# Turning keys and queries by VectorE block transposes and DRAM transfers in place of TensorE transposes, in a hybrid attention and recurrence layer

## The chip, the core and the metric

The kernel runs on one core of a Trainium2 chip. The core has TensorE (PE in the profile; its weight loads are PEld), VectorE (DVE), ScalarE (ACT), GpSimd (POOL) and SyncE (SP), which here only issues transfers. The metric is the device time of one execution in microseconds, the median of several.

## What is computed

One layer of a hybrid encoder on 512 tokens of width 2048: a norm, one input projection, full attention with eight query and two key heads of width 128, a gated recurrence (LRU) in both directions, and an output projection with the residual. Cut to what matters here:

```python
h = rms_norm(x, norm_w)
proj = jnp.einsum('bsd,de->bse', h, w_in)
q, k, v, g_attn, xr, g_lru = jnp.split(proj, SPLITS, axis=-1)
# attention_group
q = rms_norm(q.reshape(B, S, N_HEADS, HEAD_DIM), q_norm_w)     # 8 heads of 128
k = rms_norm(k.reshape(B, S, N_KV_HEADS, HEAD_DIM), k_norm_w)  # 2 heads of 128
q, k = apply_axial_rope(q, tables), apply_axial_rope(k, tables)
s = jnp.einsum('bkgqd,bksd->bkgqs', qb, k_t) * scale           # all 512 keys
p = jax.nn.softmax(s, axis=-1)
out = jnp.einsum('bkgqs,bksd->bkgqd', p, v_t)
# hybrid_layer
mixed = concatenate([rms_norm(attn_out, attn_norm_w) * silu(g_attn),
                     rms_norm(lru_out, lru_norm_w) * silu(g_lru)], axis=-1)
return x + jnp.einsum('bse,ed->bsd', mixed, w_out)
```

Everything is float32.

## The kernel before

**Arithmetic.** Every large product is three matmuls on a high and a low part of each operand (`mm3`, L151 to L154). A high part is a rounded copy (`nc.scalar.copy`, ScalarE), a low part the difference (`nc.vector.tensor_sub`, VectorE). So for each weight tile `wr` ScalarE makes `wh` (L216) and VectorE `wl` (L217).

**Stages.** TensorE goes through the input projection in groups of 512 columns: the LRU's inputs (two groups), then keys and values (one), queries (two: heads 0 to 3, heads 4 to 7), the gates (four), and then the output projection, which a seven-product scheme computes (L906). A group takes eight chunks of weights of 512 KB; a chunk is four steps of six matmuls. The weights are loaded by SP into a ring of three. The generators of the groups are the fill: `weave(fill, chain)` takes the next n steps of the fill whenever the chain of other work yields n. TensorE's instructions stand in exactly this order; those of VectorE, ScalarE and SP are put in order by the scheduler, with priorities (`high_priority`), and in the attention SP's order is by hand too.

**Keys and queries.** A projected group is evacuated with tokens on the partitions (`evac_tok`, L513), normed and turned by rope in place (`norm_rope`, L530 to L539). The scores need the head's width on the partitions. `turn` makes that with four TensorE transposes of 128x128 into one PSUM bank (L550), and `split_ps` makes the high and low part from there (L554, L555). For the keys that happens inside the second query group, between its steps; for a query head at the first tile of the head before it, head 0 at the start of the attention.

**Attention.** `attention` runs over 32 units (8 heads, 4 tiles of 128 queries). A unit: scores in three matmuls, maximum (L600), exponential (L602), reciprocal, a product on GpSimd (L604), and a 32x32 block transpose on VectorE into `u` (L605). Every two units the block-transposed weights go to DRAM and come back in four reads, which completes the transposition (`moved`: L613 to `pd`, L620 to `pt`); then they are split into `ph` and `pl` (L624). The values of a head (L152 to L154 with `ph`, `pl` and `v`) come `NT + LATE` units after its first scores. BEGIN steps of the gates' projection go ahead of the first unit, two follow each. The projections of the gates are evacuated by L392 into `ev`.

**The LRU's sum.** `group_rstd` and `rows` turn the LRU's sum of squares into a row for all partitions: a matmul with ones (L700), a copy (L704), GpSimd, a split (L281, L282), two diagonals (L284), and a matmul (L290) that TensorE reaches four steps later, inside the second query group.

Of the kernel before, what the change touches and what calls it, by code (L numbers as in the profile page):

```python
# [11 lines left out]
F32 = mybir.dt.float32  # L12
# [5 lines left out]
P = 128  # L18
SEQ = 512
DM = 2048  # L20
KT = DM // P
NT = SEQ // P
HD = 128
NH = 8
NKV = 2
G = NH // NKV
# [16 lines left out]
WARM, WARM2 = 14, 5  # L43


BEGIN, STEPS, LATE = 10, 2, 3


H = 256


B = 32
NQ = P // B
# [9 lines left out]
def hybrid_kernel(  # L63
# [20 lines left out]
    nc = tc.nc  # L84
# [28 lines left out]
    dram = ctx.enter_context(tc.tile_pool(name="dram", bufs=1, space=bass.MemoryType.DRAM))  # L113
# [3 lines left out]
    def nm(s):  # L117
        cnt[0] += 1
        return f"{s}_{cnt[0]}"
# [10 lines left out]
    def at(tag, bufs, shape, dt=F32):  # L130
        return pools["att"].tile([P, *shape], dt, tag=tag, bufs=bufs, name=nm(tag))

    def ev(dt=F32):

        for pool, n in (("lru", 4), ("qkv", 8), ("fin", 4)):
            if pool in pools:
                return pools[pool].tile([P, SEQ], dt, tag="ev", bufs=n, name=nm("ev"))

# [3 lines left out]
    def mm():  # L142
        return ps.tile([P, SEQ], F32, tag="mm", name=nm("mm"))

    def const(shape, name, dt=F32):
        return cp.tile(list(shape), dt, tag=name, name=name)

    def f(ap):
        return ap.bitcast(F32)
# [7 lines left out]
    ident = const([P, P], "ident")  # L157
# [110 lines left out]
    def rsqrt_mean(dst, src, n, width):  # L268

        nc.gpsimd.tensor_scalar(dst, src, 1.0 / n, EPS, op0=ALU.mult, op1=ALU.add)  # L270
        last_pool[0] = nc.gpsimd.tensor_tensor(dst, dst, nhalf[:, :width], op=ALU.pow).ins
# [73 lines left out]
    def weave(fill, chain):  # L345

        for n in chain:
            for _ in range(n):
                next(fill, None)

    def drain(fill):
        for _ in fill:
            pass
# [124 lines left out]
    def lru_squares():  # L478

        hsum = pools["rot"].tile([P, 2, SEQ], F32, tag="hsum", name="hsum")  # L480
        nc.scalar.activation(hsum, hp[0], AF.Square)
        for pair in hp[1:]:
            yield 2
            sq = pools["rot"].tile([P, 2, SEQ], F32, tag="hsq", bufs=1, name=nm("hsq"))
            nc.scalar.activation(sq, pair, AF.Square)
            nc.vector.tensor_add(hsum, hsum, sq)
        sums["l"] = hsum[:, 0, :]
        nc.gpsimd.tensor_add(sums["l"], sums["l"], hsum[:, 1, :])
# [18 lines left out]
    def evac_tok(acc, tile_of):  # L507

        res = []
        with tc.high_priority():  # L510
            for t in range(NT):
                e = tile_of()
                nc.scalar.activation(e, acc[t], AF.Identity, scale=rstd[:, t : t + 1])  # L513
                res.append(e)
        return res

    def norm_rope(es, nh, tab):

        es = [e[:, : nh * HD].rearrange("p (h d) -> p h d", d=HD) for e in es]
        rs = []  # L520
        for e in es:
            r = pools["rot"].tile([P, nh], F32, tag=f"rr{nh}", bufs=NT, name=nm("rr"))
            for h in range(nh):
                sq = pools["rot"].tile([P, HD], F32, tag="sh", bufs=1, name=nm("sh"))
                nc.scalar.activation(sq, e[:, h, :], AF.Square, accum_out=r[:, h : h + 1])
            rsqrt_mean(r, r, HD, nh)
            rs.append(r)
        for t, (e, r) in enumerate(zip(es, rs)):
            sq = pools["rot"].tile([P, nh, HD], F32, tag="sq", bufs=2, name=nm("sq"))
            nc.vector.tensor_mul(e, e, r[:, :, None].broadcast_to([P, nh, HD]))  # L530
            for s in range(2):
                nc.vector.tensor_mul(
                    sq.rearrange("p h (a s d) -> p h a s d", s=2, d=32)[:, :, :, s, :],
                    e.rearrange("p h (a s d) -> p h a s d", s=2, d=32)[:, :, :, 1 - s, :],
                    tab[:, t, 1, :].rearrange("p (a s d) -> p a s d", s=2, d=32)[:, None, :, s, :]
                    .broadcast_to([P, nh, 2, 32]),
                )
            nc.vector.tensor_mul(e, e, tab[:, t, 0, :][:, None, :].broadcast_to([P, nh, HD]))
            nc.vector.tensor_add(e, e, sq)  # L539
        return es  # L540

    kth, ktl = [None] * NKV, [None] * NKV
    vh = [None] * NT
    vl = [None] * NT

    def turn(rot, h):

        pt = mm()
        for t in range(NT):
            nc.tensor.transpose(pt[:, t * P : (t + 1) * P], rot[t][:, h, :], ident)  # L550
        return pt

    def split_ps(pt, hi, lo):
        nc.scalar.copy(hi, pt)  # L554
        nc.vector.tensor_sub(lo, pt, f(hi))  # L555

    def kv(es):
        rot = norm_rope(es, NKV, rk)
        yield 20
        opened("wx", "right")  # L560
        for t in range(NT):
            vv = es[t][:, NKV * HD :]
            vt = aside(
                lambda *a: pools["qkv"].tile(*a, tag="v", bufs=NT, name=nm("v")), 2 * NKV * HD // H
            )
            vh[t], vl[t] = vt[:, 0, :], vt[:, 1, :]
            nc.scalar.copy(vh[t], vv)
            nc.vector.tensor_sub(vl[t], vv, f(vh[t]))
        yield from lru_squares()
        for h in range(NKV):  # L570
            yield (16, 4)[h]
            kt = pools["qkv"].tile([P, 2, SEQ], F32R, tag="kt", bufs=NKV, name=nm("kt"))
            kth[h], ktl[h] = kt[:, 0, :], kt[:, 1, :]
            split_ps(turn(rot, h), kth[h], ktl[h])
        r = group_rstd(sums["l"], "r_l", NB * P)
        yield 4
        rows(
            gbc, r,
            lambda: pools["rope"].tile([P, NT, P], F32R, tag="kv", bufs=NT, name=nm("kv")),
        )  # L580

    def turned(rot, h):

        q = at("q", 2, (2, SEQ), F32R)
        split_ps(turn(rot, h), q[:, 0, :], q[:, 1, :])
        return q[:, 0, :], q[:, 1, :]

    pts = {}

# [58 lines left out]
            nc.scalar.activation(sq, av, AF.Square)  # L648
            nc.gpsimd.tensor_add(asum, asum, sq)

    def attention(rots):

        with tc.high_priority(AHEAD):
            qs = {0: turned(rots[0], 0)}
        yield BEGIN
        last, units = NH * NT, {}
        for i in range(last + NT + LATE):
            h, t = divmod(i, NT)
            if i < last:
                if t % 2 == 0:  # L660
                    u = at("u", 4, (NQ, NT, 2, B))
                first = pts[h - 2][2:] if h > 1 and t == 1 else ()
                weights(qs[h], h // G, t, u, first)
                if t == 0 and h + 1 < NH:
                    qs[h + 1] = turned(rots[(h + 1) // G], (h + 1) % G)
                if t % 2:
                    units[i] = moved(u, t // 2, pts.setdefault(h, []))
            for j in (i - 1, i - 3):
                if j in units:
                    next(units[j])  # L670
            j = i - NT - LATE
            if j >= 0 and j % NT == NT - 1:
                values(j // NT, *pts.pop(j // NT)[:2])
            yield STEPS + (last <= i < last + NT)
# [59 lines left out]
    def aside(tile_of, n):  # L734

        t = tile_of([P, n * H + 16], F32R)
        return t[:, 8 : 8 + n * H].rearrange("p (n e) -> p n e", e=H)
# [308 lines left out]
    for step in proj_feat(C_XR, a1, first, given):  # L1046
# [8 lines left out]
        c, e = step  # L1055
# [17 lines left out]
    fill = proj_feat(C_XR + SEQ, a2)  # L1073
# [9 lines left out]
    fill = with_sums(fill, 8, 16)  # L1083
    weave(fill, lru_half(0, a1))
    drain(fill)
    rq, rk = rope_consts()
# [11 lines left out]
    closed("lru")  # L1098
    opened("rot", "left")
    opened("qkv", "right")  # L1100
    rots = []

    def q_proj(c0, acc):
        yield from proj_tok(c0, acc)
        rots.append(norm_rope(evac_tok(acc, ev), G, rq))

    def both():
        yield from q_proj(C_Q, a4)
        yield from q_proj(C_Q + SEQ, a5)

    fill = with_sums(both(), 3)
# [3 lines left out]
    closed("rot", "rope", "wx")  # L1115
    sums["a"] = const([P, SEQ], "asum")
    opened("att", "right")

    late = []
    chunks_ = iter(  # L1120
# [4 lines left out]
    def fetch():  # L1125
        for at_ in itertools.islice(chunks_, 1):
            fetched.append(wload(w_in, *at_))
# [18 lines left out]
            else:  # L1146
                late.extend(evac_bc(acc))

    for _ in range(3):
        fetch()  # L1150
    fill = with_sums(gates(), 2)
    with tc.manual_schedule(engines={mybir.EngineType.SP}):
        weave(fill, attention(rots))
    closed("att", "qkv")
    opened("fin", "right")

# [38 lines left out]
    acc = []  # L1195
    wsums = last_sums()
    fill = with_sums(proj_feat(C_GA + SEQ, acc, take=take), 1, 8, 8 + 2 * NP)
# [74 lines left out]
```

## Time and profile before

| | |
|---|---|
| time, median of 3 | 642.65 us (642.48 to 643.1) |
| profiled execution: time, span | 642.37 us, 640.6 us |
| TensorE busy | 632.2 us (99%) |
| VectorE busy | 484.5 us (76%) |
| ScalarE busy | 342.8 us (54%) |
| granted TensorE clock | 0.999 |
| moved by DMA | 119.24 MB |

Matmuls are pipelined and their ends are modelled: a matmul lasts about 390 ns in the records, while the next begins 230 ns behind it. What TensorE loses is therefore read from the distance of the starts. Idle time of another engine costs nothing in itself.

### The profile page before, as it was taken

The page shows a single profiled execution, that of the slowest core. Times are in us where ns is not written, and L with a number is a line of the kernel's source. Part 1 is how long each engine was busy: PE and PEld are TensorE (multiplying, and loading weights), DVE is VectorE, ACT ScalarE, POOL GpSimd, SP SyncE. Part 2 cuts the span into 40 slices and gives each one's busy share as a digit, 9 for nine tenths or more (in the row PEclk, how much of TensorE's full clock was granted, in tenths as well). Part 3 has the DMA queues.
Part 4 walks back from the last instruction along what each step waited for, and adds up shares of the span by engine and source line. Part 5 has one row for each costly group of instructions (what it writes and reads, how often), then busy time and mean ns, then how long its engine had stood idle before and what let it go on. Part 6 is the DMA issues. An engine that isn't in the chain of part 4 may idle for free.

```text
span 640.6 us, 8313 instructions
## 1 busy us (share of the span) xinstructions
PE 632.2 (99%) x2835; PEld 520.2 (81%) x2835; DVE 484.5 (76%) x788; ACT 342.8 (54%) x582; POOL 102.7 (16%) x137
## 2 busy tenths in 40 slices
PE   8999999999999999999999999999999999999997
PEld 6888888888888888788788878888888888888885
DVE  5889688986688862966886788548969867787775
ACT  3534799479946723454474547426535544433441
POOL 0010210112003631522122221101210001010010
PEclk9999999999999999999999999999999999999999
DMA  9844585759674494557567644922996676796252
GB/s 297 280 147 131 139 200 165 177 143 196 209 230 145 123 215 93 117 150 211 172 172 215 197 154 143 279 83 67 246 250 194 207 252 218 280 353 231 68 198 99
DMA packets 67836, 119.24 MB, mean 186 GB/s; under 512 B 5977, under 2 KB 24529, under 8 KB 67793
## 3 DMA queue, kind: packets, MB, share of 16 engines
q1 hardware_dynamic: 59760, 100.87, 49.3%
q0 software_dynamic: 7712, 17.31, 14.3%
q10 hardware_dynamic: 320, 0.53, 0.3%
q8 instruction: 22, 0.36, 0.2%
q14 instruction: 22, 0.17, 0.1%
HBM read 106.10 MB, written 33.55 MB: 218 GB/s over the span
## 4 chain that ended last, share of the span: by engine, by line
PE 89%; DVE 4%; DMA 3%; ACT 1%; SPq 1%; issue 1%; POOL 1%; DVEq 0%; ACTq 0%
PE pj L152 18%; PE pj L153 18%; PE pj L154 18%; PE mm L906 13%; PE pj L906 10%; PE mm L153 3%; PE mm L154 3%; PE mm L152 3%; DMA wr<-in_w_in_dram 3%; PE mm L242 1%; PE pj L310 1%; DVE pl L624 1%; SPq L620 1%; DVE wl L217 1%; PE mm L550 0%
## 5 line engine op out<-in xcount | busy, mean ns | idle before, releaser
L152 PE MATMUL pj<-x,wh 128*128 128x512 f32 x376 | 148.0, 394 | 0.0
L154 PE MATMUL pj<-x,wl 128*128 128x512 f32 x376 | 146.7, 390 | 0.0
L153 PE MATMUL pj<-x,wh 128*128 128x512 f32 x376 | 146.7, 390 | 0.0
L216 ACT CAST wh<-wr 128x512 fp32r<-128x512 f32 x143 | 85.4, 619 | 82.1 <-PE pj L154 26.0
L217 DVE TENSOR_TENSOR wl<-wr,wh 128x512 fp32r<-128x512 f32 x144 | 96.4, 700 | 31.6 <-ACT wh L216 29.3
L758 ACT CAST wh<-wr 128x1024 fp32r<-128x1024 f32 (+1 forms) x72 | 60.7, 860 | 74.3 <-PE mm L906 37.7
L759 DVE TENSOR_TENSOR wl<-wr,wh 128x1024 fp32r<-128x1024 f32 (+1 forms) x72 | 68.7, 984 | 27.1 <-ACT wh L758 27.0
L154 PEld LDWEIGHTS pj<-x,wl 128*128 128x128 f32 x376 | 70.6, 188 | 15.1
L153 PEld LDWEIGHTS pj<-x,wh 128*128 128x128 f32 x376 | 70.6, 188 | 14.8 <-DVE x L245 0.3
L152 PEld LDWEIGHTS pj<-x,wh 128*128 128x128 f32 x376 | 70.6, 188 | 14.6
L152 PE MATMUL pj<-wh,x 128*128 128x512 f32 x192 | 74.9, 390 | 0.0
L154 PE MATMUL pj<-wh,x 128*128 128x512 f32 x192 | 74.7, 389 | 0.0
L153 PE MATMUL pj<-wl,x 128*128 128x512 f32 x192 | 74.7, 389 | 0.0
L782 POOL DMA_DIRECT2D t<-in_w_out_dram x40 | 33.6, 916 | 134.7 <-DMA t<-in_w_out_dram 95.9
L906 PE MATMUL mm<-wh,ml 128*128 128x512 f32 x128 | 49.8, 389 | 0.0
L906 PE MATMUL mm<-wh,mh 128*128 128x512 f32 x128 | 49.8, 389 | 0.0
L906 PE MATMUL mm<-wl,mh 128*128 128x512 f32 x128 | 49.8, 389 | 0.0
L154 PEld LDWEIGHTS pj<-wh,x 128*128 128x128 f32 x192 | 36.0, 188 | 7.5
L152 PEld LDWEIGHTS pj<-wh,x 128*128 128x128 f32 x192 | 36.0, 188 | 7.5
L602 ACT ACTIVATE p<-mm,mx 128x512 f32<-128x512 f32 x32 | 22.0, 689 | 37.6 <-DVE mx L600 36.6
L153 PEld LDWEIGHTS pj<-wl,x 128*128 128x128 f32 x192 | 36.1, 188 | 7.4
L604 POOL TENSOR_SCALAR p<-p,sm 128x512 f32<-128x512 f32 x32 | 22.3, 698 | 95.5 <-DVE sm L603 95.5
(204 smaller groups left out, 1054.0 us busy)
## 6 DMA issues: line engine op xcount, KB each, us to landing
wr<-in_w_in_dram SPq DMA_DIRECT2D x71, 512.0 KB, 4.4
wr<-in_w_out_dram SPq DMA_DIRECT2D x24, 512.0 KB, 5.1
t<-in_w_out_dram POOLq DMA_DIRECT2D x40, 256.0 KB, 6.7
wr<-t SPq DMA_DIRECT2D x40, 256.0 KB, 5.3
pd<-u SPq DMA_DIRECT2D x16, 512.0 KB, 3.0
pt<-pd SPq DMA_DIRECT2D x64, 128.0 KB, 3.3
t<-in_w_out_dram SPq DMA_DIRECT2D x24, 256.0 KB, 4.8
t<-t SPq DMA_DIRECT2D x16, 256.0 KB, 5.7
```

Source lines behind the costliest of these rows:

```text
L152: nc.tensor.matmul(acc, lh, rh, start=start, stop=False)
L153: nc.tensor.matmul(acc, lh, rl, start=False, stop=False)
L154: nc.tensor.matmul(acc, ll, rh, start=False, stop=stop)
L216: copy(hi, raw[:, k, :])
L217: nc.vector.tensor_sub(lo, raw[:, k, :], f(hi))
L242: nc.tensor.transpose(pt[:, t * P : (t + 1) * P], xc[:, t, ks], ident)
L602: nc.scalar.activation(p, sc, AF.Exp, bias=mx, accum_out=sm)
L604: last_pool[0] = nc.gpsimd.tensor_scalar(p, p, sm, 0.0, op0=ALU.mult, op1=ALU.add).ins
L758: nc.scalar.copy(hi[:, to], b)
L759: nc.vector.tensor_sub(lo[:, to], b, f(hi[:, to]))
L782: nc.gpsimd.dma_start(dst, src, accum_op=ALU.add)
L906: nc.tensor.matmul(dst[s], lh[:, ts_], rh, start=i == 0 and j == 0, stop=i == 7 and j == 2)
```

## The change

`turn` and `split_ps` go. In their place, for two heads at a time:

- `sent` makes 32x32 block transposes on VectorE (one of 128x256 for each of the four token tiles) into a tile, which SP writes to DRAM (`qd`, 512 KB).
- `landed` reads it back in four transfers of 128 KB on SP's queue, with the blocks in their places (`lq`).
- `split_head` makes the high and low part from that tile, now in SBUF.

The keys are sent right behind their norm. The first query group is sent and read back before the second is projected; the second is sent in the first two units of the attention, into buffers of `u`, and read back in heads 1 and 3. There are five such trips. Besides, `ev` has 4 buffers in place of 8, BEGIN is 11 in place of 10, the attention's tiles are allocated in a fixed order ahead, and the first gate weights are loaded behind the last read of the first query group.

```diff
-BEGIN, STEPS, LATE = 10, 2, 3
+BEGIN, STEPS, LATE = 11, 2, 3
...
-        for pool, n in (("lru", 4), ("qkv", 8), ("fin", 4)):
+        for pool, n in (("lru", 4), ("qkv", 4), ("fin", 4)):
...
-    def turn(rot, h):
-
-        pt = mm()
-        for t in range(NT):
-            nc.tensor.transpose(pt[:, t * P : (t + 1) * P], rot[t][:, h, :], ident)
-        return pt
-
-    def split_ps(pt, hi, lo):
-        nc.scalar.copy(hi, pt)
-        nc.vector.tensor_sub(lo, pt, f(hi))
+    asides, last_landed = [], [None]
+
+    def sent(es, nh, *us):
+
+        us = us or [
+            pools["rot"].tile([P, NQ, 2, NT, B], F32, tag="uq", bufs=2, name=nm("uq"))
+            for _ in range(nh // 2)
+        ]
+        for n, u in enumerate(us):
+            for t, e in enumerate(es):
+                nc.vector.transpose(
+                    u[:, :, :, t, :].rearrange("p b h r -> p h b r"),
+                    e[:, 2 * n : 2 * n + 2].rearrange("p h (b c) -> p h b c", c=B),
+                )
+            aside_ = dram.tile([P, NQ, 2 * SEQ // NQ], F32, name=nm("qd"), tag="qd", bufs=5)
+            yield
+            nc.sync.dma_start(aside_, u.rearrange("p b h t r -> p b (h t r)"))
+            asides.append(aside_)
+
+    def landed(aside_):
+
+        to = pools["qkv"].tile([P, NQ, 2, NT, B], F32, tag="lq", bufs=2, name=nm("lq"))
+        src = aside_.rearrange("(i c) b x -> b c i x", c=B)
+        for b in range(NQ):
+            last_landed[0] = nc.sync.dma_start(
+                to[b * B : (b + 1) * B].rearrange("p i h t r -> p i (h t r)"), src[b]
+            ).ins
+        return to
+
+    def split_head(pair, k, hi, lo):
+        src = pair[:, :, k]
+        hi, lo = (v.rearrange("p (t i r) -> p i t r", t=NT, i=NQ) for v in (hi, lo))
+        nc.scalar.copy(hi, src)
+        nc.vector.tensor_sub(lo, src, f(hi))
...
     def kv(es):
-        rot = norm_rope(es, NKV, rk)
+        drain(sent(norm_rope(es, NKV, rk), NKV))
+        pair = landed(asides.pop(0))
         yield 20
...
-            split_ps(turn(rot, h), kth[h], ktl[h])
+            split_head(pair, h, kth[h], ktl[h])
...
     def attention():
         with tc.high_priority(AHEAD):
-            qs = {0: turned(rots[0], 0)}
+            for h in range(2):
+                turned(h)
         yield BEGIN
...
-                if t == 0 and h + 1 < NH:
-                    qs[h + 1] = turned(rots[(h + 1) // G], (h + 1) % G)
+                if t == 0 and 0 < h < NH - 1:
+                    turned(h + 1)
...
+            if i < 2:
+                es = [e[:, 2 * i : 2 * i + 2] for e in rot]
+                writes.append(sent(es, 2, at("u", 4, (NQ, 2, NT, B))))
+                next(writes[i])
+            elif i < 4:
+                drain(writes[i - 2])
+            if t == 2 and h % 2 and asides:
+                next_pair()
...
     def both():
         yield from q_proj(C_Q, a4)
+        drain(sent(rot, G))
+        for _ in range(2):
+            next_pair()
         yield from q_proj(C_Q + SEQ, a5)
...
-    for _ in range(3):
-        fetch()
+    with tc.issue_after(last_landed[0]):
+        for _ in range(3):
+            fetch()
```

The new VectorE instructions also change how the scheduler orders the rest. VectorE, inside the second query group, where the LRU's sum is made into rows (`r_l`, `part`, `kv`), before:

```order
L539 TENSOR_TENSOR ev_2088<-ev_2088,sq_2152 128x512
L217 TENSOR_TENSOR wl_2383<-wr_2376,wh_2382 128x512
L555 TENSOR_TENSOR kt_2255<-mm_2256,kt_2255 128x512
L217 TENSOR_TENSOR wl_2414<-wr_2411,wh_2413 128x512
L217 TENSOR_TENSOR wl_2418<-wr_2411,wh_2417 128x512
L704 COPY r_l<-mm_2307 128x4
L281 CAST part_2351<-r_l 128x4
L555 TENSOR_TENSOR kt_2299<-mm_2300,kt_2299 128x512
L282 TENSOR_TENSOR part_2352<-r_l,part_2351 128x4
```

and with the change, where L704 is L746 and L555 is L579:

```order
L556 STREAM_TRANSPOSE uq_2170<-ev_2100 128x2x4x32
L556 STREAM_TRANSPOSE uq_2171<-ev_2096 128x2x4x32
L556 STREAM_TRANSPOSE uq_2171<-ev_2098 128x2x4x32
L556 STREAM_TRANSPOSE uq_2171<-ev_2100 128x2x4x32
L579 TENSOR_TENSOR kt_2330<-lq_1760,kt_2330 128x4x4x32
L217 TENSOR_TENSOR wl_2440<-wr_2437,wh_2439 128x512
L217 TENSOR_TENSOR wl_2444<-wr_2437,wh_2443 128x512
L746 COPY r_l<-mm_2333 128x4
L281 CAST part_2377<-r_l 128x4
L282 TENSOR_TENSOR part_2378<-r_l,part_2377 128x4
```

The transposes of the first query group and the second key's subtraction now stand ahead of the copy.

VectorE ahead of the values of head 0 (`pl` is the low part of its weights, `ev` the evacuated gate projection, `mx` a maximum), before:

```order
L217 TENSOR_TENSOR wl_2896<-wr_2889,wh_2895 128x512
L392 TENSOR_TENSOR ev_3122<-pj_2605,rbc 128x512
L624 TENSOR_TENSOR pl_2857<-pt_2927,ph_2856 128x4x4x64
L392 TENSOR_TENSOR ev_3124<-pj_2606,rbc 128x512
L600 TENSOR_REDUCE mx_3029<-mm_3025 128x1
```

and with the change, where L624 is L651:

```order
L392 TENSOR_TENSOR ev_3142<-pj_2636,rbc 128x512
L632 STREAM_TRANSPOSE u_3024<-p_3032 128x4x4x32
L392 TENSOR_TENSOR ev_3144<-pj_2637,rbc 128x512
L392 TENSOR_TENSOR ev_3146<-pj_2638,rbc 128x512
L651 TENSOR_TENSOR pl_2895<-pt_2965,ph_2894 128x4x4x64
L627 TENSOR_REDUCE mx_3078<-mm_3074 128x1
```

Three evacuations stand ahead of it in place of one.

SP's queue with the change, in the query groups (before, these rows are the loads L205 alone):

```order
L205 DMA wr_2472<-in_w_in_dram 128x2x512
L562 DMA qd_2176<-uq_2170 128x1024
L562 DMA qd_2182<-uq_2171 128x1024
L570 DMA lq_2184<-qd_2176 32x4x256 x4
L570 DMA lq_2189<-qd_2182 32x4x256 x4
L205 DMA wr_2598<-in_w_in_dram 128x2x512
```

The load of the first gate weights, the last row, has moved behind two writes and eight reads.

More of the change, by code (lines that the diff above doesn't have):

```diff
@@ L580, in kv, with turned @@
         )
-    def turned(rot, h):
+    qs = {}
+    def turned(h):
         q = at("q", 2, (2, SEQ), F32R)
-        split_ps(turn(rot, h), q[:, 0, :], q[:, 1, :])
-        return q[:, 0, :], q[:, 1, :]
+        qs[h] = q[:, 0, :], q[:, 1, :]
+        split_head(pairs[h // 2], h % 2, *qs[h])
     pts = {}
@@ L649, in values, with next_pair, attention @@
             nc.gpsimd.tensor_add(asum, asum, sq)
-    def attention(rots):
+    pairs, rot = [], []
+    def next_pair():
+        pairs.append(landed(asides.pop(0)))
+    def attention():
         with tc.high_priority(AHEAD):
-            qs = {0: turned(rots[0], 0)}
+            for h in range(2):
+                turned(h)
         yield BEGIN
+        writes = []
         last, units = NH * NT, {}
@@ L1100, in hybrid_kernel @@
     opened("qkv", "right")
-    rots = []
     def q_proj(c0, acc):
         yield from proj_tok(c0, acc)
-        rots.append(norm_rope(evac_tok(acc, ev), G, rq))
+        rot[:] = norm_rope(evac_tok(acc, ev), G, rq)
     def both():
         yield from q_proj(C_Q, a4)
+        drain(sent(rot, G))
+        for _ in range(2):
+            next_pair()
         yield from q_proj(C_Q + SEQ, a5)
@@ L1117, in hybrid_kernel @@
     opened("att", "right")
+    for shape, tag, bufs in (
+        ([P, SEQ], "p", 3),
+        ([P, 2, SEQ], "q", 2),
+        ([P, NQ, NT, 2, B], "u", 4),
+        ([P, NT, 2, NQ, H // NQ], "ph", 1),
+        ([P, NT, 2, NQ, H // NQ], "pl", 1),
+        ([P, NQ, NT, H // NQ], "pt", 2),
+        ([P, 32], "pad", 1),
+    ):
+        pools["att"].tile(shape, F32, tag=tag, bufs=bufs, name=nm(tag))
     late = []
@@ L1147, in gates @@
                 late.extend(evac_bc(acc))
-    for _ in range(3):
-        fetch()
+    with tc.issue_after(last_landed[0]):
+        for _ in range(3):
+            fetch()
     fill = with_sums(gates(), 2)
     with tc.manual_schedule(engines={mybir.EngineType.SP}):
-        weave(fill, attention(rots))
+        weave(fill, attention())
     closed("att", "qkv")
```

## The prediction

> **What bounds the kernel now.** I read the page first, then what TensorE (PE) waits for, then its groups by line, then the timelines of PE and VectorE (DVE) around the transposes and around each wait of PE.
>
> The page's first two lines: span, then each engine's busy time, share and instructions.
>
> ```profile
> span 640.6 us, 8313 instructions
> PE 632.2 (99%) x2835; PEld 520.2 (81%) x2835; DVE 484.5 (76%) x788; ACT 342.8 (54%) x582; POOL 102.7 (16%) x137
> ```
>
> PE is never without work for long. The table of waits for PE alone (engine and line, releaser, us in total, times, longest) holds three, in two rows, that touch this change:
>
> ```profile
> PE mm L153 <- DVE pl L624: 1.5, 2, 1.0
> PE mm L154 <- DVE q L555: 0.7, 1, 0.7
> ```
>
> So time is gained by taking instructions off PE, as long as nothing that PE then waits for comes later. The transposes of keys and queries are 40 instructions of one line (groups by line; busy us, mean ns):
>
> ```profile
> L550 PE MATMUL mm<-ident,ev 128*128 128x128 f32 x32 | 4.8, 272 | 0.0
> L550 PE MATMUL mm<-ident,kv 128*128 128x128 f32 x8 | 1.2, 272 | 0.0
> ```
>
> Their 272 ns overlap, so the price is read from start to start, in the timeline of PE around one block of four:
>
> ```profile
> 222.20 0.39 PE L153 MATMUL pj<-wl,x 128*128 128x512 f32 x1
> ...
> 223.11 0.40 PE L154 MATMUL pj<-wh,x 128*128 128x512 f32 x1
> 223.34 0.60 PE L550 MATMUL mm<-ident,kv 128*128 128x128 f32 x4
> 223.70 0.47 PE L152 MATMUL pj<-wh,x 128*128 128x512 f32 x1
> 224.01 0.40 PE L153 MATMUL pj<-wl,x 128*128 128x512 f32 x1
> 224.24 0.40 PE L154 MATMUL pj<-wh,x 128*128 128x512 f32 x1
> ```
>
> From 222.20 to 223.11 lie four steps, 0.2275 us each. From 223.11 to 224.24 there would be three steps, 0.68 us, without the block; there are 1.13. A block costs 0.45 us, part of it in the slower restart behind it (0.31 instead of 0.23).
>
> **The change, part by part.**
>
> *Removed from PE.* Ten blocks (two key heads, eight query heads) of 0.45 us: 4.5 us, all of it on the path, since PE is what ends last. The row's 272 ns times 40 would be 10.9 us, but most of that overlaps. [...]
>
> *The wait before the first scores.* PE's third matmul of head 0 waits for the low part of the query:
>
> ```profile
> 269.95 0.39 PE L153 MATMUL mm<-kt,q 128*128 128x512 f32 x1
> 271.03 0.50 PE L154 MATMUL mm<-kt,q 128*128 128x512 f32 x1 [0.69 <-DVE q L555]
> 271.37 0.60 PE L550 MATMUL mm<-ident,ev 128*128 128x128 f32 x4
> ```
> ```profile
> 270.29 0.68 DVE L555 TENSOR_TENSOR q<-mm,q 128x512 fp32r<-128x512 f32 x1
> ```
>
> It costs 1.08 - 0.23 = 0.85, and 0.11 of slow restart (0.34 to the next matmul): 0.96 us. DVE reaches this subtraction when it is through with the norm and rope of the second query group, and the order of the change has it in the same place. But BEGIN goes from 10 to 11 steps of six matmuls. Counted from the transposes that open the stage:
>
> ```profile
> 255.61 0.60 PE L550 MATMUL mm<-ident,ev 128*128 128x128 f32 x4
> ```
>
> 11 x 6 x 0.2275 = 15.0 us, so the scores start at 270.6 on the old clock and the third matmul is due at 271.1; DVE ends at 270.97. The wait shrinks to between 0 and 0.3: I take 0.15, a gain of 0.8.
>
> *The wait before head 4's (and head 0's) values.* These two are where the evacuation of a gate projection (L392) stands ahead of the low part of the weights (L624) on DVE. PE, then DVE:
>
> ```profile
> 376.08 0.40 PE L152 MATMUL mm<-ph,v 128*128 128x512 f32 x1
> 377.45 0.50 PE L153 MATMUL mm<-pl,v 128*128 128x512 f32 x1 [0.98 <-DVE pl L624]
> ```
> ```profile
> 375.57 0.69 DVE L392 TENSOR_TENSOR ev<-pj,rbc 128x512 f32<-128x512 f32 x1 [0.48 <-PE pj L154]
> 376.18 1.22 DVE L624 TENSOR_TENSOR pl<-pt,ph 128x1024 fp32r<-128x1024 f32 x1
> ```
>
> The evacuation waits for the projection's matmul just ahead of the scores, so L624 starts only when the first value matmul does, and PE loses 1.37 - 0.23 = 1.14 and 0.11 of restart: 1.25 us. At head 0 it is shorter now:
>
> ```profile
> 307.15 0.40 PE L152 MATMUL mm<-ph,v 128*128 128x512 f32 x1
> 308.02 0.50 PE L153 MATMUL mm<-pl,v 128*128 128x512 f32 x1 [0.47 <-DVE pl L624]
> ```
>
> 0.87 - 0.23 + 0.11 = 0.75 us, since only an evacuation that was ready stands ahead of it. With one step more in BEGIN, the order of the change puts three evacuations ahead of L624 at head 0, the last of them fed just before the scores, as at head 4 now. I take 1.25 for both heads: +0.5 us.
>
> *Added to DVE.* 20 block transposes of 128x256, not in the trace. Nearest rows: the 128x512 transpose and a 128x256 product.
>
> ```profile
> L605 DVE STREAM_TRANSPOSE u<-p 128x512 f32<-128x512 f32 x30 | 21.2, 707 | 12.0 <-POOL p L604 11.8
> L532 DVE TENSOR_TENSOR sq<-ev,rq 128x256 f32<-128x256 f32 x16 | 6.3, 418 | 0.1
> ```
>
> Each lies between 0.35 (half of 707) and 0.71; I take 0.42, by the equal size: 1.7 us for the keys, 3.4 for each query group. The subtractions stay. DVE's room (stretch, PE, PEld, DVE, ACT, POOL busy, clock, DMA share, GB/s):
>
> ```profile
> 220.00:230.00 10.00, 10.00 (x52) 8.34 (x50) 8.19 (x16) 3.18 (x6) 4.58 (x6) 1.00 0.84 174
> 270.00:280.00 10.00, 9.31 (x43) 7.44 (x42) 6.21 (x12) 4.74 (x9) 2.37 (x4) 1.00 0.73 158
> ```
>
> The second query group's transposes fall into 272 to 282, where DVE has 3.8 us in ten free. They delay head 0's later maxima, but not what PE waits for next.
>
> *What the first group's transposes push.* They stand ahead of the small chain that turns the LRU's sum into rows (L704, POOL, L281, L284), and PE waits for its end at L290:
>
> ```profile
> 226.94 1.28 DVE L217 TENSOR_TENSOR wl<-wr,wh 128x512 fp32r<-128x512 f32 x2
> 230.69 0.16 DVE L704 COPY r_l<-mm 128x4 f32<-128x4 f32 x1 [2.47 <-PE mm L700]
> 232.30 0.17 DVE L281 CAST part<-r_l 128x4 fp32r<-128x4 f32 x1 [1.44 <-POOL r_l L271]
> 233.04 1.29 DVE L284 TENSOR_TENSOR kv<-ident,part 128x512 fp32r<-128x512 f32 x2
> ```
> ```profile
> 236.08 0.62 PE L290 MATMUL mm<-kv,ones_r 128*128 128x512 f32 x2
> ```
>
> Now DVE is through with its older work at 228.2 and idles 2.5 us before the copy. Before that point come seven or eight transposes (3.1), both key subtractions instead of one (0.6), and up to 0.5 because ScalarE casts the keys between the squares that feed the norm: 232.4. The copy then starts 1.7 us later than now, less the second key subtraction (0.6) that leaves the chain. Its end moves from 234.3 to 235.4. PE comes to L290 0.9 us earlier, two blocks being gone: 235.2. Now the chain has 1.7 us to spare; then it is about even. The cost lies between 0 and 2 us (2 if the key's trip through DRAM, which ScalarE's cast then waits for, lands late): I take 0.5.
>
> *Added transfers.* Five trips of 512 KB out and 4 x 128 KB back, on SP's queue. Nearest rows (KB each, median us to landing):
>
> ```profile
> pd<-u SPq DMA_DIRECT2D x16, 512.0 KB, 3.0
> pt<-pd SPq DMA_DIRECT2D x64, 128.0 KB, 3.3
> ```
>
> A trip is 6 to 8 us with the issues. The keys' has ten; the first queries are back long before the scores; the second group's are issued a head or more ahead. Queued behind the first queries' eight reads is the load of the first gate weights, now issued at 226.45, split on DVE at 239.74 and used by PE at 255.97:
>
> ```profile
> 226.45 0.37 SPq L205 DMA_DIRECT2D wr<-in_w_in_dram  x1
> 239.74 0.68 DVE L217 TENSOR_TENSOR wl<-wr,wh 128x512 fp32r<-128x512 f32 x1
> 255.97 0.48 PE L152 MATMUL pj<-x,wh 128*128 128x512 f32 x1
> ```
>
> I put its issue at about 237, its landing at 242 to 246: 9 us of cover left, so nothing. Without that cover every us late would be one on PE.
>
> The sum: -4.5 - 0.8 + 0.5 + 0.5 = -4.3 us. The profiled execution took 642.37 us around its span of 640.6, 0.28 below the median of 642.65; 642.37 - 4.3 = 638.1, and by the median **638.4 us**.
>
> **The rivals.** *Half of it is given back.* VectorE's longer order makes PE wait the full 2 us at L290, and 0.75 at the first scores as well: -4.5 - 0.1 + 0.5 + 2 = -2.1, 640.5 us. For it: that chain is even by my count. Against: DVE idles 2.5 us there now.
>
> *DVE falls behind at every head.* Each head's values need L624 in time, and without an evacuation the cover is short: at head 3 it ended at 358.58 and PE used it at 359.27.
>
> ```profile
> 357.37 1.21 DVE L624 TENSOR_TENSOR pl<-pt,ph 128x1024 fp32r<-128x1024 f32 x1
> 359.27 0.40 PE L153 MATMUL mm<-pl,v 128*128 128x512 f32 x1
> ```
>
> A head is now 0.45 us shorter on PE and no shorter on DVE. If L624 came 1.6 us later against PE, 0.9 beyond this cover, at each of eight heads, 7.2 us would be lost: -4.3 + 7.2 = +2.9, **645.6 us**. It decides the sign from 0.55 us a head on (4.3 / 8). Against it: DVE is 62% busy at 270 to 280. [...]
>
> *The gain is hidden.* Other waits take the 4.5 us up and nothing changes: 642.6. PE's waits here come to 2.2 us in all in the table, so little speaks for it. *More is gained:* if all three waits vanished, -4.5 - 0.96 - 0.75 - 1.25 = -7.5, 635.2.
>
> **How the numbers follow.** My forecast, 637 to 640, has 0.60; half given back 0.17; more gained 0.04; hidden 0.06; DVE behind 0.13. Faster: 0.60 + 0.17 + 0.04 = 0.81, the same 0.06, slower 0.13; 0.2% (1.3 us) is about what a measurement of this kernel can tell. From 636.2 to 641.8 lies all of the forecast, nearly all of the half and a piece of the others: 0.8.
>
> **What would show it.** L550 gone; PE's steps unchanged at 0.2275; no wait over 0.3 at the first scores; 1.25 at the values of heads 0 and 4; at L290's place (L291 is its copy) 0 to 2. Waits of PE for pl at other heads, or for weights behind the queries' reads, would prove me wrong.

## The result and the profile after

| | before | after |
|---|---|---|
| median of 22 executions each, us | 642.79 (642.14 to 644.0) | 642.62 (639.9 to 645.18) |
| ratio to before | 1 | 0.9992 [0.998, 1.0004] |
| profiled execution: time, span, us | 642.37, 640.6 | 643.89, 641.8 |
| its granted TensorE clock | 0.999 | 0.997 |

No difference, where 4.3 us less was forecast. The executions of after fall in two, eleven at a granted clock of 0.999 or 1.000 with a mean of 641.1 us and eleven at 0.998 or less with 643.7, and the profiled one is of the second kind.

First the page, then the table of what TensorE (PE) waits for (engine and line, releaser, us in total, times, longest):

```profile
span 641.8 us, 8300 instructions
PE 630.6 (98%) x2795; PEld 517.3 (81%) x2795; DVE 492.6 (77%) x808; ACT 340.7 (53%) x582; POOL 102.8 (16%) x137
```
```profile
PE mm L153 <- DVE pl L651: 2.8, 4, 1.0
PE mm L154 <- DVE q L579: 2.2, 1, 2.2
...
PE pj L152 <- ACT ev L513: 0.2, 1, 0.2
PE pj L154 <- DVE wl L217: 0.2, 1, 0.2
```

The 40 transposes are gone. In their place the first scores wait 2.2 instead of 0.7, the low part of the weights (pl, L651, which was L624) is waited for four times instead of twice, and two small waits are new. The line numbers of after are higher: q L579 was L555.

PE around the first scores (start, duration, line, tiles, idle before and its releaser):

```profile
271.90 0.39 PE L153 MATMUL mm<-kt,q 128*128 128x512 f32 x1
274.49 0.50 PE L154 MATMUL mm<-kt,q 128*128 128x512 f32 x1 [2.20 <-DVE q L579]
274.83 0.40 PE L152 MATMUL pj<-x,wh 128*128 128x512 f32 x1
...
276.00 0.63 PE L154 MATMUL pj<-x,wl 128*128 128x512 f32 x1
276.42 0.63 PE L152 MATMUL pj<-x,wh 128*128 128x512 f32 x1
...
279.41 0.40 PE L153 MATMUL mm<-kt,q 128*128 128x512 f32 x1
```

The wait itself costs 2.47 us: 2.59 from start to start, less one step of 0.2275, and 0.11 of slow restart. What follows it is a second loss: from 276.00 to 279.41 lie eight steps of 0.427 us instead of 0.2275, 3.41 us for 1.82, 1.6 lost. The row of this stretch has a granted clock of 0.83 (columns as in the prediction: stretch, PE, PEld, DVE, ACT, POOL busy, clock, DMA share, GB/s):

```profile
230.00:240.00 10.00, 10.00 (x48) 8.29 (x48) 8.49 (x17) 1.25 (x2) 4.55 (x6) 1.00 0.95 206
240.00:250.00 10.00, 10.00 (x46) 8.28 (x45) 2.61 (x3) 0.00 (x0) 3.26 (x4) 1.00 1.07 252
270.00:280.00 10.00, 7.80 (x28) 5.95 (x27) 6.51 (x12) 3.19 (x5) 2.35 (x3) 0.83 0.98 213
```

The other thing to see here is ScalarE (ACT) at 240 to 250: it did nothing at all. Its own timeline, and SP's queue, say why:

```profile
230.33 1.32 SPq L562 DMA_DIRECT2D qd<-uq  x2
237.44 4.01 SPq L570 DMA_DIRECT2D lq<-qd  x8
241.69 3.77 SPq L205 DMA_DIRECT2D wr<-in_w_in_dram  x3
```
```profile
252.54 1.14 ACT L216 CAST wh<-wr 128x512 fp32r<-128x512 f32 x2 [18.33 <-DMA wr<-in_w_in_dram]
...
255.20 0.68 ACT L513 ACTIVATE ev<-pj,rstd 128x512 f32<-128x512 f32 x1
```

The two writes of the first queries, issued from 230.33, let the eight reads start only at 237.44: 7 us for the first trip out. Behind the reads stand the first gate weights, issued at 241.69 instead of 226.45, and there they took 10.9 us to land, until the cast at 252.54 that waits for them (the median of their kind is 4.2). In ScalarE's order the casts of these weights stand ahead of the evacuation of the second query group (L513), and in the 18.33 us before the first of them it ran nothing. So the evacuation starts at 255.20 (251.72 in before), and norm, rope and the subtraction that the first scores need follow it:

```profile
272.54 1.29 DVE L217 TENSOR_TENSOR wl<-wr,wh 128x512 fp32r<-128x512 f32 x2
273.75 1.29 DVE L579 TENSOR_TENSOR q<-lq,q 128x512 fp32r<-128x512 f32 x2
```

The pair ends near 275, the half that PE waits for at 274.4, where before had 270.97. Last, the values at heads 0 and 1; the waits at heads 4 and 3 are of the same sizes:

```profile
311.90 0.50 PE L153 MATMUL mm<-pl,v 128*128 128x512 f32 x1 [1.00 <-DVE pl L651]
328.99 0.50 PE L153 MATMUL mm<-pl,v 128*128 128x512 f32 x1 [0.38 <-DVE pl L651]
```

The account of the two profiled executions, each loss measured from start to start less 0.2275 and with its 0.11 of slow restart, in us:

| | after less before |
|---|---|
| transposes on PE (L550) | -4.5 |
| wait before the first scores, 0.96 to 2.47 | +1.5 |
| eight steps at 0.427 behind it | +1.6 |
| values, head 0 (0.75 to 1.27); head 4 stays (1.25 to 1.27) | +0.5 |
| values, heads 1 and 3 (new, 0.65 and 0.66) | +1.3 |
| new waits at 210.4 (0.47), 255.9 (0.40), 263.2 (0.45) | +1.3 |
| first matmul of the projections, at 5.96 before and 6.33 after | +0.4 |
| PE's other steps from 260 to 400 us, mean 230.1 ns before and 228.0 after | -1.2 |
| sum; the spans differ by | +0.9; +1.2 |

The last 0.3 is spread over small steps. Two lines need a word. Only before shows a wait for the first weights (PE pj L310 <- DVE wh L216, 0.5), but after is no faster for lacking it: PE reaches that matmul only at 6.33. And the prediction took PE's steps for 0.2275 everywhere, when in before the matmuls of the scores stand further apart: at head 0 they start at 306.45, 306.69 and 306.92 with the next matmul at 307.15, and in after at 306.42, 306.65, 306.88 and 307.10. On the mean over the units the first score starts 0.232 us behind the matmul ahead of it, the next two follow after 0.241 and 0.232 and the projection after 0.236, each of which is 0.227 in after. So the change took about 5.7 us off PE and not 4.5. Every kernel below that turns on PE has the longer steps and every one that turns through DRAM the shorter; why is not shown.

### The profile page after: what moved, and what is told of

It reads as the page before. It is cut to its first block, busy times and chain, and to the rows that moved or that the text cites. A ratio compares the mean times of both kernels' runs of the same rounds, so it can differ in the third digit from the quotient of the medians.

```text
span 641.8 us, 8300 instructions
## 1 busy us (share of the span) xinstructions
PE 630.6 (98%) x2795; PEld 517.3 (81%) x2795; DVE 492.6 (77%) x808; ACT 340.7 (53%) x582; POOL 102.8 (16%) x137
## 4 chain that ended last, share of the span: by engine, by line
PE 74%; DVE 11%; ACT 6%; DMA 4%; issue 2%; POOL 2%; SPq 0%; DVEq 0%; ACTq 0%; POOLq 0%
PE mm L948 13%; PE pj L152 13%; PE pj L153 13%; PE pj L154 13%; PE pj L948 10%; PE mm L153 3%; DVE wl L217 3%; PE mm L154 3%; PE mm L152 3%; DMA wr<-in_w_in_dram 2%; ACT wh L216 1%; ACT sh L525 1%; DVE pl L651 1%; PE mm L242 1%; DMA pt<-pd 1%
## 5 line engine op out<-in xcount | busy, mean ns | idle before, releaser
L216 ACT CAST wh<-wr 128x512 fp32r<-128x512 f32 x143 | 85.7, 618 | 105.6 <-PE pj L153 37.5
L217 DVE TENSOR_TENSOR wl<-wr,wh 128x512 fp32r<-128x512 f32 x144 | 99.1, 715 | 30.5 <-ACT wh L216 29.8
L631 POOL TENSOR_SCALAR p<-p,sm 128x512 f32<-128x512 f32 x32 | 23.7, 745 | 95.5 <-DVE sm L630 95.5
```

The costliest lines, as they stand in the source:

```text
L216: copy(hi, raw[:, k, :])
L217: nc.vector.tensor_sub(lo, raw[:, k, :], f(hi))
L631: last_pool[0] = nc.gpsimd.tensor_scalar(p, p, sm, 0.0, op0=ALU.mult, op1=ALU.add).ins
```

## The experiments

Each run is compared with runs of before on the same chip: 642.58 us for experiments 1 and 2 and the first two of experiment 3, 642.77 for the other two of experiment 3 and experiments 4 and 5, 642.6 for experiment 6.

**1. The gate weights no longer behind the reads.** After, with one line changed:

```
-    with tc.issue_after(last_landed[0]):
+    if True:
         for _ in range(3):
             fetch()
```

> The change, but the first gate weights are no longer held behind the last read of the first query group: on SP's queue the first of them goes ahead of the two writes, the second ahead of the eight reads, the third among them. Queue theory: in the changed kernel these weights landed at 252.5 instead of about 231, ScalarE stood 18.3 us before their cast, and the evacuation of the second query group, which comes behind it on ScalarE, began at 255.2 instead of 251.7; so here the evacuation begins at about 252, the first scores wait 0 to 0.5 us instead of 2.4, TensorE's half clock behind them (3 us long, 1.6 us lost) is gone, the granted clock is 0.999 or 1.000 in every execution, and the time is 638.5 to 639.5 us. VectorE theory: the added block transposes make the subtraction late in any case; the wait stays at 2 us or more and the time at 642.

Measured: 638.89 us (638.13 to 638.98), ratio 0.9941 [0.9928, 0.9953], clock 0.999 to 1.000 in every execution.

```profile
228.35 0.37 SPq L205 DMA_DIRECT2D wr<-in_w_in_dram  x1
230.56 1.33 SPq L562 DMA_DIRECT2D qd<-uq  x2
```
```profile
252.01 0.69 ACT L513 ACTIVATE ev<-pj,rstd 128x512 f32<-128x512 f32 x1 [1.42 <-PE pj L154]
```
```profile
PE mm L153 <- DVE pl L651: 2.8, 4, 1.0
...
```

The first weights leave at 228.35 ahead of the writes, the evacuation comes at 252.01 and waits for PE alone, and the wait at the first scores, the slow steps and the waits at 255.9 and 263.2 are gone. Of the forecast's 4.3 us, 3.7 are there; the one line had taken them back. The four waits for pl stay.

**2. The DMA engines emptied a little.** After, with the side transfers for the partial sums of the output projection's weights moved from the second query group (223 to 249 us) into the gates:

```
-    fill = with_sums(both(), 3)
+    fill = with_sums(both(), 3, 0, 32)
```

> The change, but GpSimd's and SP's side transfers for the output projection's weight sums stop halfway through the two query groups and go on in the gates: the queue's order of weights and reads is that of the change, only the other traffic at 230 to 255 us is gone. Bandwidth theory: the weights came late because all 16 DMA engines were full there (share 0.95 to 1.07); with free engines the first gate weights land within 6 us of their issue at about 237, the first scores wait at most 0.5 us, time 638.5 to 640. Order theory: they come late because SP issues them behind the reads; issue moves by 4 us at most, ScalarE is held to about 247, which would still be ahead of the evacuation, so the wait goes as well, but the landing stays over 8 us behind the issue. VectorE theory: no change, 642.

Measured: 644.12 us (641.42 to 644.71), ratio 1.0023 [1.0013, 1.0033]. The stretches, and the place where the traffic went:

```profile
240.00:250.00 10.00, 10.00 (x46) 8.29 (x45) 3.51 (x5) 1.87 (x3) 0.00 (x0) 1.00 0.43 151
290.00:300.00 10.00, 10.00 (x46) 8.29 (x45) 6.41 (x12) 4.27 (x8) 4.43 (x6) 1.00 1.08 283
300.00:310.00 10.00, 7.60 (x30) 5.65 (x30) 7.81 (x14) 4.31 (x9) 1.90 (x3) 0.94 1.06 268
```
```profile
306.61 0.51 PE L152 MATMUL mm<-ph,v 128*128 128x512 f32 x1 [1.64 <-ACT ph L651]
307.87 0.50 PE L153 MATMUL mm<-pl,v 128*128 128x512 f32 x1 [0.76 <-DVE pl L651]
```

With a share of 0.43 at 240 to 250 the weights, still held behind the reads, were issued at 236.25 and landed at about 241, and nothing waited at the first scores. So the order in the queue and the full engines were both needed for the wait. But the traffic then filled 290 to 310, head 0's weights came back late, and the half-speed steps followed there. The total says nothing for or against the order.

**3. The start of the scores.** BEGIN is the number of steps of six matmuls ahead of the scores. After with 13 for 11; before with 11 for 10; after as in experiment 1 with 9 for 11; before with 9 for 10.

> The change with 13 steps of the gates ahead of the first scores in place of 11, that is 2.7 us more of TensorE's own work over the wait there. If the wait is the loss, it shrinks from 2.4 to between 0 and 0.4 us, no half clock follows, granted clock 0.999 or more in every execution, and the time falls by 2.5 to 4 us to 638.5 to 640. At the values of heads 0 and 4 four gate evacuations come ahead of the weights' low part, of which the last is fed 1.4 us earlier against the scores: waits there of 0 to 1.3 us. If TensorE's slow stretch has another cause than the wait (power, the dense run before), the clock stays at 0.996 in half of the executions.

> The kernel before with BEGIN at 11 in place of 10 and nothing else: the part of the change that costs no transfer. By the prediction's count the wait before the first scores falls from 0.96 to 0 to 0.3 us and the one before head 0's values grows from 0.75 to 1.25: 0.3 us faster, 642.3 to 642.6, within what can be told apart. If the order of VectorE moves more than that, waits appear at other heads and it is slower by 1 us or more.

> The same kernel (weights not held back) with BEGIN 9 instead of 11: the scores start two steps (2.73 us) earlier while VectorE's subtraction of the first query still ends near 271.2, so TensorE should wait about 2.7 us at the first scores with the DMA engines not full. Theory of the half clock (a wait of over 2 us by itself brings TensorE's steps to 0.43 us for some 3 us in many executions): steps of 0.43 behind the wait, granted clock at or below 0.998, another 1.6 us lost. Rival (the slower steps came from the traffic of the DMA engines): no step of 0.43, clock 0.999. For the values of heads 0 and 4 the new order has one evacuation instead of three between the two halves of the low part; if this is what made them wait, 2.5 us come back there. So: 640.8 with the half clock and without these waits, 639.2 with neither, 643.3 with both.

> The kernel before with BEGIN 9 instead of 10, nothing else: no transfers are added anywhere. The first scores come 1.37 us earlier and the subtraction they need does not, so the wait there should grow from 0.96 to 2.3 us. Theory of the half clock (it is the wait): steps of 0.43 us behind it in a good part of the executions, granted clock at or below 0.998 in these, 644 to 645.6. Rival (it is the traffic): no such steps, clock 0.999, 643.2 to 644.0 (the lower end if the wait before head 0's values, 0.75, goes since only one evacuation stands ahead of it).

| | us | ratio to before | first scores | waits of PE for the values |
|---|---|---|---|---|
| after, BEGIN 13 | 647.1 (645.74 to 648.78) | 1.0074 [1.006, 1.0087] | none | all of heads 0 to 5 |
| before, BEGIN 11 | 641.45 (641.08 to 641.83) | 0.9982 [0.9973, 0.9991] | none | head 4 |
| experiment 1, BEGIN 9 | 644.85 (642.68 to 645.36) | 1.0026 [1.0014, 1.0038] | 2.7 | all of heads 0 to 5 |
| before, BEGIN 9 | 647.42 (646.73 to 648.45) | 1.0076 [1.0064, 1.0089] | 0.8 and 1.4 | all of heads 0 to 5 |

None of the four times came where it was expected, although the half-speed steps came in both kernels with BEGIN 9. The rows of what PE waits for in these kernels, in the order of the table's first two and last:

```profile
PE mm L153 <- DVE pl L651: 5.7, 6, 1.4
PE mm L152 <- ACT ph L651: 2.5, 2, 1.7
```
```profile
PE mm L153 <- DVE pl L624: 1.0, 1, 1.0
```
```profile
PE mm L153 <- DVE pl L624: 3.4, 6, 1.0
PE mm L154 <- DVE q L555: 1.2, 1, 1.2
```

BEGIN 11 alone makes before 1.1 us faster: its waits at the first scores and at head 0 both vanish, so a longer BEGIN alone does not put head 0's low part behind. BEGIN 9 and 13 bring a wait for the weights at every one of six heads, in before too, where nothing is turned on VectorE; with 13, PE waits for ScalarE's high part (ph) as well, at heads 1 and 5. Which phase between scores and projections does this stays open. With BEGIN 9 in experiment 1 a single evacuation stands between the two halves of pl at heads 0 and 4, and the wait there is the same 1.27 us. So it is not the number of evacuations that counts, but the last one, which waits for PE. For the half-speed steps the last kernel is the clean one, since it has no transfer that before has not:

```profile
269.17 0.50 PE L152 MATMUL mm<-kt,q 128*128 128x512 f32 x1 [0.60 <-ACT q L554]
...
271.09 0.77 PE L154 MATMUL mm<-kt,q 128*128 128x512 f32 x1 [1.19 <-DVE q L555]
...
273.37 0.63 PE L154 MATMUL pj<-x,wl 128*128 128x512 f32 x1
273.79 0.63 PE L152 MATMUL pj<-x,wh 128*128 128x512 f32 x1
```

Two waits close together, 2.1 us of lost steps, and then steps of 0.427 again. In experiment 1 with BEGIN 9, after a wait of 2.7 us, there were seven such steps. So they can follow a wait, and the added transfers are not needed for them.

**4. What the blocks on PE cost.** Before, each block of four transposes issued twice:

```
-        for t in range(NT):
+        for t in 2 * list(range(NT)):
             nc.tensor.transpose(pt[:, t * P : (t + 1) * P], rot[t][:, h, :], ident)
```

> The kernel before with each block of four TensorE transposes issued twice into the same target: 40 transposes more, nothing else. By the starts in the trace (a block costs 0.45 us, of which four issue distances of 0.107 us): +4.3 us, less up to 0.4 of the wait before the first scores: 646.5 to 647.0. By the durations (40 x 0.272 us): +10.9 us, 653.5. If the blocks were hidden: 642.6.

Measured: 645.57 us (645.55 to 645.66), ratio 1.0043 [1.0028, 1.0059]: +2.8. PE around one block:

```profile
286.89 1.03 PE L550 MATMUL mm<-ident,ev 128*128 128x128 f32 x8
287.68 0.48 PE L152 MATMUL pj<-x,wh 128*128 128x512 f32 x1
```

From the block to the next matmul lie 0.79 us; in before the same distance is 0.36 (223.34 to 223.70). The second four cost 0.43 to 0.44, ten times that 4.4, and two waits of before are not in this trace: the one at the first scores (0.96) and the one at head 0 (0.75). 4.4 - 1.7 = 2.7. The starts had the price right; I had counted too little of the waits that a slower PE makes disappear.

**5. The waits at heads 1 and 3.** Experiment 1, with the reads of the third and fourth pair at another unit:

```
-            if t == 2 and h % 2 and asides:
+            if t == 0 and h in (2, 3):
                 next_pair()
```

> The kernel after with the first gate weights no longer held behind the queries' reads (as in the run before of 638.89 us), and with the reads of the third and fourth pair of queries issued at the first unit of heads 2 and 3 instead of the third unit of heads 1 and 3. Theory (the 0.67 us that TensorE waits for the low part of the weights at heads 1 and 3 come from the order that the scheduler gives VectorE around these reads; in the new order the first half's subtraction stands four to five instructions earlier at both heads): both waits go, -1.3 us: 637.3 to 637.9. Rival (VectorE is behind at these heads since it carries the transposes, whatever its order): the waits stay or move to the next head, 638.6 to 639.2.

Measured: 637.78 us (637.39 to 637.88), ratio 0.9921 [0.9907, 0.9935], 1.1 below experiment 1 (1.3, each against its own before). Where VectorE takes head 1's two halves of pl, experiment 1 and then this kernel:

```profile
320.59 1.19 DVE L651 TENSOR_TENSOR pl<-pt,ph 128x1024 fp32r<-128x1024 f32 x1
...
322.90 1.22 DVE L651 TENSOR_TENSOR pl<-pt,ph 128x1024 fp32r<-128x1024 f32 x1
```
```profile
316.07 1.18 DVE L651 TENSOR_TENSOR pl<-pt,ph 128x1024 fp32r<-128x1024 f32 x1
...
322.16 1.22 DVE L651 TENSOR_TENSOR pl<-pt,ph 128x1024 fp32r<-128x1024 f32 x1
```

The first half moves from 320.59 to 316.07, out of the crowd before the values. Head 3's wait is gone, head 1's falls from 0.67 to 0.45, head 2 gets 0.24; the rest of the 1.1 is the small wait at 210, which is not in this trace. So of the 1.3 at heads 1 and 3 half came back: the order made these waits in good part, and what is left at heads 1 and 2 was not explained.

**6. The waits at heads 0 and 4.** Experiment 5, and before with BEGIN 11, each with the evacuations of the first two gate projections placed behind the low part of that head:

```
         his[2:] = [nc.scalar.copy(hi, pt).ins, nc.vector.tensor_sub(lo, pt, f(hi)).ins]
+        lows.append(his[3])
...
-                todo = gate(evac_bc(acc), hp[2 * n : 2 * n + 2], row, None)
+                with tc.issue_after(lows[8 * n + 1]):
+                    evs = evac_bc(acc)
+                todo = gate(evs, hp[2 * n : 2 * n + 2], row, None)
```

> The kernel of the run before (gate weights not held back, pair reads at heads 2 and 3: 637.78 us), with the four evacuations of each of the first two gate projections placed behind the low part of the weights of head 0 and of head 4 on VectorE. Theory (what TensorE waits for there, 1.27 us at each of the two heads, is only that an evacuation fed by the matmul just ahead of the scores stands in front of this subtraction): both waits go, -2.5 us: 635.0 to 635.6. Rival (VectorE has no room there, and the work that is moved back makes the next head's subtraction or the next projection late by as much): 637.2 to 638.

> The kernel before with BEGIN 11 (alone 641.45 us, with only head 4's wait left) and the same placing of the evacuations: the best of before without the transfers. Theory: head 4's wait of 1.26 us goes, 640.0 to 640.4, and the distance to the same arrangement with the turning through DRAM is what turning on TensorE costs, 4.5 us (ten blocks of 0.45): 4.3 to 5. Rival (the distance is smaller, since part of what the changed kernel gained in these runs was the arrangement's): under 3.5.

Measured: 635.51 us (635.33 to 636.15), ratio 0.989 [0.9876, 0.9903], and 640.06 us (639.82 to 640.83), ratio 0.9962 [0.9948, 0.9976]. VectorE at head 0 in experiment 1, where each evacuation (L392) waits for PE and pl for the evacuation, and then with the new placing:

```profile
303.83 0.69 DVE L392 TENSOR_TENSOR ev<-pj,rbc 128x512 f32<-128x512 f32 x1 [0.22 <-PE pj L154]
305.19 0.69 DVE L392 TENSOR_TENSOR ev<-pj,rbc 128x512 f32<-128x512 f32 x1 [0.67 <-PE pj L154]
305.80 1.22 DVE L651 TENSOR_TENSOR pl<-pt,ph 128x1024 fp32r<-128x1024 f32 x1
```
```profile
302.27 1.18 DVE L651 TENSOR_TENSOR pl<-pt,ph 128x1024 fp32r<-128x1024 f32 x1
303.37 1.87 DVE L392 TENSOR_TENSOR ev<-pj,rbc 128x512 f32<-128x512 f32 x3
```

The waits went in both kernels, at heads 0 and 4 in the first and at head 4 in the second, where BEGIN 11 had taken head 0's away. In the first, 0.4 came back at head 1 (0.45 to 0.85), so 2.1 us of 2.5 were gained, each against its own before. The two kernels now have the same arrangement of BEGIN and evacuations, one turning through DRAM and one on PE, and are 640.06 - 635.51 = 4.55 us apart.

This net difference is ten times 0.45 partly by chance. In the trace of the kernel that turns on PE no wait is left but the one for the constants (L160); in the other PE still loses 0.46 at 210, 0.85 at head 1, 0.24 at head 2 and 0.56 at 557, 2.1 in all. Against that stand its shorter steps, 227.9 ns for 230.6 from 260 to 400 us, about 1.6 us. Together that is 4.5 + 1.6 - 2.1 = 4.0, and the spans of the two profiled executions differ by 4.0 (638.1 and 634.1). The blocks alone are priced by experiment 4 and by the distances of the starts, at 0.43 to 0.45 each.

## Why the prediction was wrong

- **The blocks, -4.5: right.** L550 is gone, and experiment 4 shows 0.43 to 0.44 a block. That PE's steps would stay unchanged at 0.2275 was wrong in the change's favour: those of the scores became shorter, 1.2 us that the sum did not have.
- **The added transfers, 0: the step that failed.** "I put its issue at about 237, its landing at 242 to 246: 9 us of cover left, so nothing." The issue was at 241.69 and the landing at about 252.5. Two things in this step were wrong. The trip was taken from medians (3.0 us out) where the first went out in 7, with the DMA engines at 0.95 and 1.07 of their share; that the stretch is full could be read beforehand, since before had 1.04 at 230 to 240 already. And the cover was counted to PE's use of the weights at 255.97, when the nearest thing behind the load was ScalarE's cast, with the evacuation of the second query group queued behind it.
- **The wait before the first scores, 0.96 to 0.15: wrong for that reason alone.** It became 2.47. In experiment 1 nothing is waited for there, and before with BEGIN 11 shows the same. What I counted for BEGIN was right.
- **Steps at half speed, not in the sum:** 1.6 us in the profiled execution, and nothing of them in before. Waits were priced at their own length plus 0.11 of restart; the last section has where that fails.
- **Heads 0 and 4, 1.25 each: right in size** (1.27, both), and the cause was the evacuation, as experiment 6 shows. That BEGIN's extra step brings it to head 0 was wrong: in before it takes head 0's wait away.
- **"DVE behind at every head", a rival at 0.13:** it came in small, at heads 1 and 3, 0.65 and 0.66 each. I had left it out of the sum; the cause was in good part where the pair reads put the first subtraction (experiment 5), with VectorE 62% busy by my count and 77% over the span.
- **The rows chain, 0 to 2, taken 0.5: nearer 0.** The copy came at 232.98 for my 232.4, the chain ended just when PE arrived (both at 236.1, for my 235.4 and 235.2), and PE did not wait at L290.
- **The transposes on VectorE, 0.42 each:** 0.42 for the first query group, 0.44 for the keys.

```profile
L556 DVE STREAM_TRANSPOSE uq<-ev 128x256 f32<-128x256 f32 x8 | 3.0, 416 | 0.0
```

The total came out at the rival "the gain is hidden", 642.6, to which I gave 0.06, and in kind by its mechanism: other waits took up what PE gained. They were not those that I counted against it, though, but new ones, and experiments 1, 5 and 6 show that most of them are not inherent in the change. That they came to just the size of the gain is chance. With PE as the bound, turning through DRAM is 4.55 us faster in this kernel than turning on PE (experiment 6: 635.51 and 640.06) once its transfers delay nothing, the shorter steps of the scores included. Not settled: why the wait at 210 comes and goes between the kernels, why the executions at the lower clock are 2.6 us longer when one stretch of slow steps explains 1.6 (only one of them was traced), the longer steps of the scores in before, and BEGIN 9 and 13.

## What to carry to other kernels

A transfer put ahead of loads in one queue can make them late, and with them the engine that takes them next: here the gate weights were issued at 241.69 instead of 226.45, and ScalarE ran nothing for 18.33 us before their cast. Count the cover to the first instruction that stands behind the load on any engine, not to the final use, and do not take the trip's time from a median over the run where the DMA engines are full at that place (3.0 by the median, 7.1 and 8.3 us there). Work taken off the bounding engine is worth its issue distances (0.45 us a block here, not the sum of durations), but only as long as the other engines' queues keep the order that served the old timing; read what stands ahead of each waited-for instruction and, where it waits for the bounding engine itself, move it behind.

## What the runs showed of the hardware

- TensorE's granted clock fell to one half in four traces. In after it is 0.50 from 275.99 to 279.40, 3.41 us, and the steps are 0.427 us instead of 0.2275. In the other three the rows of ten us show it: 0.94 in experiment 2 (300 to 310, above, with steps of 0.43 from 309.00 on), and 0.83 in experiment 1 with BEGIN 9 and in before with BEGIN 9 (columns as above):

```profile
270.00:280.00 10.00, 8.73 (x31) 7.04 (x32) 5.81 (x13) 2.59 (x6) 2.10 (x3) 0.83 0.77 157
```
```profile
270.00:280.00 10.00, 8.91 (x34) 7.32 (x35) 5.46 (x10) 4.57 (x8) 1.84 (x4) 0.83 0.72 158
```

Each time PE had just lost steps to waits: 2.4 us in after, 1.8 and 1.0 in experiment 2, 2.7 in experiment 1 with BEGIN 9, 0.8 and 1.4 in before with BEGIN 9. But in after with BEGIN 13 two waits before head 1's values lose 3.2 us in all, and the clock stays at 1.00. Here are the 3.41 us with the wait in after and the 3.41 behind them, then two such stretches with the waits in after with BEGIN 13:

```profile
272.58:275.99 3.41, 1.50 (x6) 1.24 (x7) 3.14 (x6) 0.49 (x1) 1.22 (x2) 1.00 1.12 232
275.99:279.40 3.41, 3.41 (x9) 2.67 (x8) 0.86 (x2) 2.70 (x5) 1.13 (x2) 0.50 0.98 217
```
```profile
324.95:328.36 3.41, 2.08 (x10) 1.38 (x8) 3.34 (x6) 3.41 (x7) 0.00 (x0) 1.00 0.65 164
328.36:331.77 3.41, 1.94 (x7) 1.40 (x8) 3.12 (x5) 1.16 (x2) 0.00 (x0) 1.00 0.44 144
```

In after PE is idle for 1.91 us of the first stretch (by the records, whose ends are modelled), and half clock follows. With BEGIN 13 it is idle for 1.33 and 1.47 us of the two, and both have 1.00. So the time lost to waits did not decide it alone; what did is not shown.

- In after the first queries' writes of 512 KB took 7.1 and 8.3 us to land where the DMA engines' share was 0.96 (230.33 to 237.44), when the median of such writes in the attention is 3.0, and a load behind them 10.9 instead of 4.2. In experiment 2, without the side transfers, the same writes took 2.7 and 3.0 us at a share of 0.70, and the load 5.0 at 1.08. So the share alone does not give the time:

```profile
qd<-uq SPq DMA_DIRECT2D x3, 512.0 KB, 7.7
```
